# The last stage of an encoder block in program order, with operands made two steps ahead

## The chip, the cores and the metric

The kernel runs on one core of a Trainium2 chip. The metric is the device time of one execution in microseconds, the median of several. Besides, one execution is recorded by the profiler; its "span" runs from the first to the last instruction of the program. The engines are PE (TensorE, matmuls), DVE (VectorE), ACT (ScalarE), POOL (GpSimd) and SP (SyncE, which here only issues DMAs). Each engine works through its own instructions in the order that it was given, and waits at the first one that isn't ready.

## The reference, cut to what matters

One layer of an encoder: input norm, dilated attention and a recurrent branch, a merge, a norm, then SwiGLU and a last norm. The change lies in the very last product and that norm:

```python
D_MODEL = 1024; SEQ = 1024; D_FF = 2816        # all float32
def layer_norm(x, g, b):
    mu = mean(x); xc = x - mu
    return xc * rsqrt(mean(xc * xc) + 1e-5) * g + b
...
    h = layer_norm(alpha * h + merged @ w_o, ln1_g, ln1_b)
    gate, up = split(h @ w_ffn_in, 2)
    h = layer_norm(alpha * h + (silu(gate) * up) @ w_ffn_out, ln2_g, ln2_b)
```

In the last line a 1024 x 2816 matrix is multiplied by a 2816 x 1024 one.

## The kernel before, in words

**Precision.** A float32 operand is split into two float32r parts, hi and lo, with hi + lo the operand (`split`, L204 the cast, L208 the subtraction). A product of two split operands is three matmuls (`mm3`, L229 to L231): hi·hi, hi·lo, lo·hi. By default the cast is ACT's and the subtraction POOL's; for some tiles (`eng_lo="dve"`) it is DVE's.

**The last stage** (`ffn_out`) multiplies the activations g (rows by D_FF) with `w_ffn_out` in Strassen-Winograd form: each matrix is cut into 2 x 2 quarters, and seven products of sums of quarters replace eight. `OUT_ORDER` is the order of the first six, (1, 2, 6, 5, 7, 3); product 4 comes last in a loop of its own. The inner dimension of a quarter, 1408, is cut into NJ = 11 pieces of 128. A *step* is one product and one piece j: 12 matmuls (four row tiles t of 128 rows, three matmuls each) into four PSUM banks, X (`pj`) for products 1, 6, 7, 4 and Z (`sd`) for 2, 5, 3. There are 66 steps. The products accumulate on each other in the banks as the Winograd form asks: 6 on 1, 7 on 6, 4 on 7, 3 on 5.

**Operands of a step.** The activations of products 1, 2 and 6 (a11, a12, s2) lie in DRAM whole: one DMA (`graw`, three buffers under the tag `wsum`) and a split into `ghi`, `glo` (three buffers), cast on ACT, subtraction on DVE. Those of 5, 7 and 3 (s1, s3, s4) lie there split: two DMAs straight into `ghi` and `glo`. The weights come in four quarters b11, b12, b21, b22, 11 tiles of 128 x 512 (256 KB) each, and stay in SBUF. `right` makes a product's weight operand with DVE sums in place: nothing for products 1 and 2, b12−b11 and b22−b11 for 6, b21+b11 for 5 (kept for later; the operand is b11), b22−b12 for 7, b21−b22 for 3. `split` then makes `w_hi`, `w_lo` (four buffers) on ACT and POOL. During product 3 product 4's weights are split as well (`t4hi`, `t4lo`). Product 4's activations a22 come as two transfers of 704 KB per row tile (`a22h`, `a22l`), in two buffers each.

**Loads.** `at(step, ...)` hangs each bulk load on a step: weight tiles, the eight residual row tiles (`rows`, Y), the two vectors of the norm (`vector`), the first two pairs of a22 (`last_acts`). They are issued by SP, kept in program order by `queued`.

**Rows.** When a product's banks are complete, `add` adds them to the residual rows in Y, one addition per step or all at once. `finish(t)` normalises a row tile: statistics of both halves (DVE, `stats`), the power −1/2 (POOL), scale and shift (ACT, `normalise`), the multiplication by g2 (POOL, L1592), the addition of b2 (DVE, L1593) and the output DMA (L1594). Tile 7 does the last parts by halves on DVE (L1584, L1587).

**Order.** Outside what `queued` fixes, a scheduler orders each engine's instructions when the program is built: it goes by program order as priority and by its own estimate of when an instruction is ready. `add` runs in a block that raises its priority (`evac_ahead`).

**The last loop** (product 4), over t = 0 to 3: for t of 2 and 3 the a22 pair is loaded at the head of the turn; then 33 matmuls into X[t], the addition, and `finish` of three tiles in turns 0 and 1, of one in turns 2 and 3.

`out_begin`, called from the stage before, loads the first four weight tiles and three activations and splits step 0's operands.

Of the kernel before, what the change touches and what calls it, by code (L numbers as in the profile page):

```python
# [81 lines left out]
class Block:  # L82
# [1397 lines left out]
    OUT_ROWS = {1: ((0, 0),), 2: ((0, 0),), 6: ((0, 1),), 5: ((1, 1),), 7: ((1, 1),), 3: ((0, 1),)}  # L1480

    def queued(self, o, i):

        return self.tc.keep_in_program_order(self.nc.sync.dma_start(o, i))
# [4 lines left out]
    def out_block(self, t, n, j):  # L1489
        k, c = int(n[1]) - 1, int(n[2]) - 1  # L1490
        self.queued(t, self.wfo[128 * (j + NJ * k):128 * (j + NJ * k + 1), HALF * c:HALF * (c + 1)])
        return t

    def out_raw(self, p, j):
        r = self.ws.tile([128, HALF], F32, name="graw", tag="wsum", bufs=3)
        self.queued(r, self.gd[self.OUT_G[p]][j][0])
        return r

    def out_begin(self):
# [11 lines left out]
        self.begun = {(1, 0): (g, w)}  # L1511
        self.raws = {(1, j): self.out_raw(1, j) for j in (1, 2)}

    def ffn_out(self):


        nc = self.nc
        with ExitStack() as es:
            wb = es.enter_context(self.pool("fow"))
            rp = es.enter_context(self.pool("for", "right"))  # L1520
            W, Y, gains = self.W, {}, []
            halves = [slice(HALF * h, HALF * (h + 1)) for h in range(2)]

# [3 lines left out]
            def rows(t):  # L1527
                Y[t] = y = rp.tile([128, D], F32, name="y2", tag=f"y2{t}", bufs=1)
                self.queued(y, self.ahs_d[t])

            def vector(i):
                v = self.ln["2"][i]
                gains.append(rp.tile([128, D], F32, name=f"gb{i}"))
                self.queued(gains[i], bass.AP(tensor=v.tensor, offset=v.offset, ap=[[0, 128], [1, D]]))

            def acts(p, j):
                d = self.gd[self.OUT_G[p]][j]
                z = [rp.tile([128, HALF], F32R, name=f"g{n}", tag=f"g{n}", bufs=3) for n in ("hi", "lo")]
                if len(d) == 1:
                    self.split(*z, self.raws.pop((p, j), None) or self.out_raw(p, j), eng_lo="dve")  # L1540
                else:
                    for t, s in zip(z, d):
                        self.queued(t.bitcast(F32), s)
                return z

            a22 = []

            def last_acts(t, i):
                if i == 0:
                    a22.append([rp.tile([128, NJ, 128], F32R, name=f"a22{z}", tag=f"a22{z}", bufs=2) for z in "hl"])  # L1550
                self.queued(a22[t][i].bitcast(F32), self.gd["a22"][i][:, :, 128 * t:128 * (t + 1)])

            def right(p, j):
                b11, b12, b21, b22 = (W.get((n, j)) for n in ("b11", "b12", "b21", "b22"))
                if p == 1:
                    return b11
                if p == 2:
                    return b21
                if p == 6:
                    t2 = self.ws.tile([128, HALF], F32, name="wt2", tag="wkeep", bufs=3)  # L1560
                    nc.vector.tensor_sub(b11, b12, b11)
                    nc.vector.tensor_sub(t2, b22, b11)
                    return t2
                if p == 5:
                    nc.vector.tensor_add(b21, b21, b11)
                    return b11
                if p == 7:
                    nc.vector.tensor_sub(b12, b22, b12)
                    return b12
                nc.vector.tensor_sub(b21, b21, b22)  # L1570
                return b22

            def add(t, h, ps):
                with self.tc.high_priority(offset=self.evac_ahead):
                    nc.vector.tensor_add(Y[t][:, halves[h]], Y[t][:, halves[h]], ps)

            def finish(t):
                y, (g2, b2) = Y[t], gains
                mv = self.stats(rp, y, "2")
                if t == 7:  # L1580
                    for n in range(2):
                        for s in halves:
                            if n == 0:
                                nc.vector.scalar_tensor_tensor(y[:, s], y[:, s], mv[:, 0:1], g2[:, s],  # L1584
                                                               op0=OP.subtract, op1=OP.mult)
                            else:
                                nc.vector.scalar_tensor_tensor(y[:, s], y[:, s], mv[:, 2:3], b2[:, s],  # L1587
                                                               op0=OP.mult, op1=OP.add)
                                nc.sync.dma_start(self.out[128 * t:128 * (t + 1), s], y[:, s])
                else:  # L1590
                    self.normalise(rp, y, y, mv)
                    nc.gpsimd.tensor_mul(y, y, g2)  # L1592
                    nc.vector.tensor_add(y, y, b2)  # L1593
                    nc.sync.dma_start(self.out[128 * t:128 * (t + 1), :], y)  # L1594
# [22 lines left out]
            late, adds, step = {}, [], 0  # L1617
            for p in self.OUT_ORDER:
# [75 lines left out]
```

## Time and profile before

| | |
|---|---|
| timed runs | median 2212.6 us, 2210.78 to 2212.82 (3 runs) |
| profiled execution | 2210.36 us |
| its span | 2208.6 us |
| PE busy | 2048.6 us, 93% |
| DVE, ACT, POOL busy | 1380.7, 919.4, 1234.5 us |
| mean granted clock of PE | 0.97 |

The profile lists instructions by line of the kernel, engine and tile, with start times in us from the span's start. "Idle before, releaser" is the time that the engine had waited and what ended that wait. `pj` and `sd` are PSUM banks; `Wb` a weight tile, `w_raw` one of the first four; `wt` the sum b22−b11. SPq is SP's queue of DMA issues. Matmul durations overlap: the pace is read from the distances of starts.

### The profile page before, as it was taken

Reading aid. Unit: us, or ns where it says so; the run is one execution under the profiler, and the core shown is the slowest. Engines: PE = TensorE matmul, PEld = TensorE weight load, DVE = VectorE, ACT = ScalarE, POOL = GpSimd, SP = SyncE. Lnnn points to the kernel's source line nnn. Section 1 sums busy time; section 2 is a strip of 40 time slices with the busy share of each in tenths; the row PEclk is TensorE's granted clock in tenths of the full one; section 3 lists DMA queues with packets and bytes.
Section 4 is the critical chain, followed back from the end, with each engine's and each line's share of the span. In section 5 each row is a group of like instructions: output and inputs, shape, how many; then the busy total and the mean of one; then the engine's idle time right before and its main releaser. Section 6 shows DMA issues by size and latency. Waiting matters only on the chain.

```text
span 2208.6 us, 31268 instructions
## 1 busy us (share of the span) xinstructions
PE 2048.6 (93%) x10941; PEld 1685.4 (76%) x10941; DVE 1380.7 (63%) x2165; ACT 919.4 (42%) x1870; POOL 1234.5 (56%) x960
## 2 busy tenths in 40 slices
PE   4799999999999999999999999998999999988973
PEld 3678887878878888778887788786888888777862
DVE  7657645885378846776456323368688887767242
ACT  6534454433554445444553321344444344343220
POOL 3565653666446654556546653535677777555450
PEclk9899999999999999999999999999999999999996
DMA  5333442434333452435427562345344444484743
GB/s 204 103 121 106 155 137 93 137 127 154 118 109 129 131 162 92 136 116 161 133 82 270 191 210 82 125 133 181 124 154 163 146 164 151 156 288 137 244 150 96
DMA packets 296447, 324.20 MB, mean 147 GB/s; under 512 B 15905, under 2 KB 212834, under 8 KB 296290
## 3 DMA queue, kind: packets, MB, share of 16 engines
q1 hardware_dynamic: 288832, 296.81, 41.8%
q10 hardware_dynamic: 7458, 25.40, 3.0%
q8 instruction: 86, 1.41, 0.3%
q14 instruction: 71, 0.58, 0.1%
HBM read 211.78 MB, written 110.36 MB: 146 GB/s over the span
## 4 chain that ended last, share of the span: by engine, by line
PE 56%; DVE 8%; DMA 4%; issue 4%; POOL 4%; ACT 2%; SPq 0%; DVEq 0%; POOLq 0%; ACTq 0%
PE pj L229 12%; PE pj L231 12%; PE pj L230 12%; PE sd L231 5%; PE sd L229 5%; PE sd L230 5%; POOL w_lo L208 2%; PE sd L1023 1%; ACT p L801 1%; DMA a22l<-ga22l 1%; DVE p L823 1%; DVE y L1593 1%; DVE hR L984 1%; DMA wa<-in_w_in_dram 1%; DVE qd L938 1%
## 5 line engine op out<-in xcount | busy, mean ns | idle before, releaser
L208 POOL TENSOR_TENSOR w_lo<-wa,w_hi 128x512 fp32r<-128x512 f32 x276 | 387.2, 1411 | 278.9 <-ACT w_hi L204 271.3
L204 ACT CAST w_hi<-wa 128x512 fp32r<-128x512 f32 x276 | 170.1, 618 | 235.5 <-PE pj L230 169.4
L208 POOL TENSOR_TENSOR w_lo<-wsum,w_hi 128x512 fp32r<-128x512 f32 x88 | 135.6, 1551 | 78.0 <-ACT w_hi L204 41.2
L208 POOL TENSOR_TENSOR w_lo<-f_raw,w_hi 128x512 fp32r<-128x512 f32 x66 | 110.4, 1686 | 66.0 <-ACT w_hi L204 64.2
L229 PE MATMUL pj<-xt1hi,w_hi 128*128 128x512 f32 x268 | 108.9, 407 | 23.6 <-ACT xt1hi L204 16.7
L208 POOL TENSOR_TENSOR w_lo<-Wb,w_hi 128x512 fp32r<-128x512 f32 x47 | 72.5, 1545 | 73.5 <-ACT w_hi L204 71.9
L230 PE MATMUL pj<-xt1lo,w_hi 128*128 128x512 f32 x268 | 107.8, 402 | 4.5 <-DVE xt1lo L208 4.5
L231 PE MATMUL pj<-xt1hi,w_lo 128*128 128x512 f32 x268 | 107.1, 400 | 0.0
L231 PE MATMUL pj<-xb22hi,w_lo 128*128 128x512 f32 x268 | 105.0, 392 | 2.2 <-POOL w_lo L208 2.2
L229 PE MATMUL pj<-xb22hi,w_hi 128*128 128x512 f32 x268 | 105.9, 395 | 0.1
L463 POOL TENSOR_TENSOR wa<-wa,wa 128x512 f32<-128x512 f32 x46 | 64.5, 1403 | 72.3 <-DVE ws L462 59.8
L230 PE MATMUL pj<-xb22lo,w_hi 128*128 128x512 f32 x268 | 104.9, 391 | 0.0
L208 POOL TENSOR_TENSOR w_lo<-ws,w_hi 128x512 fp32r<-128x512 f32 x46 | 67.4, 1468 | 63.7 <-ACT w_hi L204 57.3
L485 ACT COPY wkeep<-pj 128x512 f32<-128x512 f32 x138 | 80.4, 583 | 11.4 <-DVE evh L377 5.9
L229 PE MATMUL pj<-xb11hi,w_hi 128*128 128x512 f32 x188 | 77.9, 416 | 5.1 <-DVE wkeep L402 3.6
L204 ACT CAST w_hi<-wsum 128x512 fp32r<-128x512 f32 x88 | 54.6, 620 | 63.9 <-PE sd L230 61.3
L388 DVE TENSOR_TENSOR evh<-wkeep,pj 128x512 f32<-128x512 f32 x48 | 32.6, 679 | 76.5 <-PE pj L231 56.4
L1393 ACT ACTIVATE fth<-fc 128x512 f32<-128x512 f32 x44 | 27.8, 633 | 125.9 <-DVE fc L1392 125.9
L229 PEld LDWEIGHTS pj<-xt1hi,w_hi 128*128 128x128 f32 x268 | 51.8, 194 | 37.1 <-ACT xt1hi L204 17.4
L231 PE MATMUL pj<-xt2hi,w_lo 128*128 128x512 f32 x188 | 74.7, 397 | 3.8 <-POOL w_lo L208 3.8
L229 PE MATMUL pj<-xt4hi,w_hi 128*128 128x512 f32 x188 | 75.9, 404 | 2.3 <-DVE evh L377 2.3
L975 ACT ACTIVATE hS<-hR,dec 128x128 f32<-128x128 f32 x112 | 44.5, 402 | 78.8 <-DVE hR L984 56.8
(416 smaller groups left out, 6717.2 us busy)
## 6 DMA issues: line engine op xcount, KB each, us to landing
wa<-in_w_in_dram SPq DMA_DIRECT2D x184, 256.0 KB, 3.0
f_raw<-in_w_ffn_in_dram SPq DMA_DIRECT2D x44, 512.0 KB, 4.3
Wb<-in_w_ffn_out_dram SPq DMA_DIRECT2D x40, 256.0 KB, 4.1
tg<-evh SPq DMA_DIRECT2D x32, 256.0 KB, 3.1
tg<-tg SPq DMA_DIRECT2D x16, 512.0 KB, 3.6
y<-ahs SPq DMA_DIRECT2D x16, 512.0 KB, 4.9
ah<-xt ACTq DMA_DIRECT2D x8, 512.0 KB, 6.6
rec<-hg ACTq DMA_DIRECT2D x8, 512.0 KB, 3.7
```

Of the source, the lines that this page charges most:

```text
L204: nc.scalar.copy(hi, src)
L208: e.tensor_sub(lo, src, hi.bitcast(F32))
L229: nc.tensor.matmul(ps, whi, xhi, start=first, stop=False, **kw)
L230: nc.tensor.matmul(ps, whi, xlo, start=False, stop=False, **kw)
L231: nc.tensor.matmul(ps, wlo, xhi, start=False, stop=last, **kw)
L388: nc.vector.tensor_add(t, add, ps)
L463: nc.gpsimd.tensor_sub(a["a21"], a["a11"], a["a21"])
L485: nc.scalar.copy(t, ps)
L801: nc.scalar.activation(z, z, AF.Exp, bias=N0[p, hd, tt:tt + 1], scale=QSCALE, accum_out=L0[p, hd, tt:tt + 1])
L823: nc.vector.tensor_scalar(z, z, W0[p, hd, tt:tt + 1], None, op0=OP.mult)
L975: nc.scalar.activation(S[:, c, :], E, AF.Copy, scale=dec[:, 1, c:c + 1])
L1393: nc.scalar.activation(th[:, s], c[:, s], AF.Tanh, scale=0.5)
```

## The change

Only the last stage is changed. What it computes, the number of instructions of each kind and their operands stay.

1. A context `in_order` chains all instructions traced inside it to the one before on the same engine, so that each engine follows program order through the whole stage; it takes the place of `queued` and of the raised priority of `add`.
2. A step's operands are made two steps ahead: in step s stand `sums(s + 2)` (its weight sum) and `prep(s + 2)` (its splits), then the bulk loads of step s, then the matmuls of step s, then one addition or statistics from the list `todo`, then the activation DMAs (`acts`) of step s + 4 where they come whole, of s + 3 where they come split.
3. The sum b12−b11 is made with product 2 in place of product 6.
4. Loads are hung on other steps: b21 at 4 + j (was 7 + j), b12 at 6 + j (16 + j), rows 0 to 3 from 15 (11), rows 4 to 7 from 32 (33), the first a22 pairs from 52 (55).
5. Statistics are taken per half: `stat(t, h)`. One half of each tile is taken between steps, after products 2 and 7; `moments` does the rest.
6. In the last loop the a22 pairs for t = 2 and 3 are issued right behind the matmuls of t = 0 and 1, ahead of those turns' outputs. `finish` returns the last addition and the output DMA as a function, which is called after the next tile's `finish`. The order of tiles is 0, 1, 4, 2, 3, 5, 6, 7.

```diff
+    @contextmanager
+    def in_order(self):
+        traced = self.nc.cur_bb.bb.instructions
+        n = len(traced)
+        yield
+        for i in traced[n:]:
+            before = self.lasts.get(i.engine)
+            if before is not None:
+                self.tc.add_manual_dep(i, before, mybir.DependencyInfo(mybir.DependencyClass.NoSync,
+                                                                       mybir.DependencyReason.DATA), reason="in_order")
+            self.lasts[i.engine] = i.name
...
+            def sums(s):
+                if not 0 <= s < len(steps):
+                    return
+                p, j = steps[s]
                 b11, b12, b21, b22 = (W.get((n, j)) for n in ("b11", "b12", "b21", "b22"))
-                if p == 1:
-                    return b11
                 if p == 2:
-                    return b21
-                if p == 6:
-                    t2 = self.ws.tile([128, HALF], F32, name="wt2", tag="wkeep", bufs=3)
                     nc.vector.tensor_sub(b11, b12, b11)
+                elif p == 6:
+                    W["t2", j] = t2 = self.ws.tile([128, HALF], F32, name="wt2", tag="wkeep", bufs=3)
                     nc.vector.tensor_sub(t2, b22, b11)
...
+            RIGHT = {1: "b11", 2: "b21", 6: "t2", 5: "b11", 7: "b12", 3: "b22"}
+
+            def prep(s):
+                if s >= len(steps) or s in ready:
+                    return
+                p, j = steps[s]
+                w = self.flat()
+                raw = self.raws.pop((p, j), None)
+                if raw is not None:
+                    g = pair()
+                    nc.scalar.copy(g[0], raw)
+                    nc.vector.tensor_sub(g[1], raw, g[0].bitcast(F32))
+                else:
+                    g = G.pop(s)
+                self.split(*w, W[RIGHT[p], j])
+                ready[s] = g, w
 
             def add(t, h, ps):
-                with self.tc.high_priority(offset=self.evac_ahead):
-                    nc.vector.tensor_add(Y[t][:, halves[h]], Y[t][:, halves[h]], ps)
+                nc.vector.tensor_add(Y[t][:, halves[h]], Y[t][:, halves[h]], ps)
+
+            def stat(t, h):
+                if t not in S:
+                    S[t] = rp.tile([128, 2, 6], F32, name="bns", tag=f"bns{t}", bufs=1)
+                nc.vector.bn_stats(S[t][:, h, :], Y[t][:, halves[h]])
...
+                self.normalise(rp, y, y, mv)
+                nc.gpsimd.tensor_mul(y, y, g2)
+                return lambda: (nc.vector.tensor_add(y, y, b2),
+                                nc.sync.dma_start(self.out[128 * t:128 * (t + 1), :], y))
...
             for j in range(NJ):
-                at(7 + j, load, "b21", j)
-                at(16 + j, load, "b12", j)
+                at(4 + j, load, "b21", j)
+                at(6 + j, load, "b12", j)
                 at(17 + j, load, "b22", j)
             for t in range(4):
-                at(11 + t, rows, t)
-                at(33 + 2 * t, rows, 4 + t)
+                at(15 + t, rows, t)
+                at(32 + 2 * t, rows, 4 + t)
             for i in range(2):
                 at(46 + 2 * i, vector, i)
                 for t in range(2):
-                    at(55 + 4 * t + 2 * i, last_acts, t, i)
+                    at(52 + 4 * t + 2 * i, last_acts, t, i)
...
+            with self.in_order():
+                acts(3)
+                prep(1)
+            for s, (p, j) in enumerate(steps):
                 bank = X if p in (1, 6, 7) else Z
-                for j in range(NJ):
-                    if (p, j) in self.begun:
-                        g, w = self.begun[p, j]
-                    else:
-                        g, w = acts(p, j), self.flat()
-                        self.split(*w, right(p, j))
-                    for f, *a in bulk.pop(step, []):
+                with self.in_order():
+                    sums(s + 2)
+                    prep(s + 2)
+                    for f, *a in bulk.pop(s, []):
                         f(*a)
-                    if p == 3:
-                        late[j] = ...
+                    if p == 3 and j:
+                        later(j - 1)
+                    g, w = ready.pop(s)
                     for t in range(4):
                         c = slice(128 * t, 128 * (t + 1))
                         self.mm3(bank[t], g[0][:, c], g[1][:, c], *w, ...)
-                    if adds and (p != 2 or j > 4):
-                        add(*adds.pop(0))
+                    if todo and (p != 2 or j >= NJ - 4):
+                        f, *a = todo.pop(0)
+                        f(*a)
+                    acts(s + (4 if steps[min(s + 4, len(steps) - 1)][0] in (1, 2, 6) else 3))
+                if j == NJ - 1:
+                    i, h = self.OUT_ROWS[p]
+                    adds = [(add, 4 * i + t, h, bank[t]) for t in range(4)]
+                    todo += adds
+                    if p in (2, 7):
+                        todo += [(stat, 4 * i + t, h) for t in range(4)]
...
+            with self.in_order():
+                later(NJ - 1)
+                for f, *a in todo:
+                    f(*a)
+                for t in range(4):
+                    for j in range(NJ):
+                        self.mm3(X[t], A[t][0][:, j, :], A[t][1][:, j, :], *late[j], False, j == NJ - 1, ...)
+                    if t < 2:
+                        for i in range(2):
+                            last_acts(2 + t, i)
+
+                    def done(r):
+                        ends.append(finish(r))
+                        if len(ends) > 1:
+                            ends.pop(0)()
+
+                    if t == 0:
+                        for r in range(4):
+                            stat(r, 1)
+                        done(0)
+                        done(1)
+                    if t == 1:
+                        done(2)
+                        done(3)
+                    add(4 + t, 0, X[t])
+                    stat(4 + t, 0)
+                    if t < 3:
+                        done(4 + t)
+                    else:
+                        ends.pop(0)()
+                        finish(7)
```

More of the change, by code (lines that the diff above doesn't have):

```diff
@@ L1 @@
 import math
-from contextlib import ExitStack
+from contextlib import ExitStack, contextmanager
 import numpy as np
@@ L1520, in ffn_out @@
             rp = es.enter_context(self.pool("for", "right"))
-            W, Y, gains = self.W, {}, []
+            W, Y, S, V, G, A, ready = self.W, {}, {}, [], {}, [], self.ready
             halves = [slice(HALF * h, HALF * (h + 1)) for h in range(2)]
+            steps = [(p, j) for p in self.OUT_ORDER for j in range(NJ)]
             def load(n, j):
@@ L1536, in acts @@
[L1536 removed]
+                V.append(rp.tile([128, D], F32, name=f"gb{i}"))
+                nc.sync.dma_start(V[i], bass.AP(tensor=v.tensor, offset=v.offset, ap=[[0, 128], [1, D]]))
+            def acts(s):
+                if s >= len(steps):
+                    return
+                p, j = steps[s]
                 d = self.gd[self.OUT_G[p]][j]
[L1538 removed]
                 if len(d) == 1:
[L1540 to L1544 removed]
@@ L1546, in ffn_out, with pair @@
-            a22 = []
+                    if (p, j) not in self.raws:
+                        self.raws[p, j] = self.out_raw(p, j)
+                    return
+                G[s] = z = pair()
+                for t, v in zip(z, d):
+                    nc.sync.dma_start(t.bitcast(F32), v)
+            def pair():
+                return [rp.tile([128, HALF], F32R, name=f"g{n}", tag=f"g{n}", bufs=3) for n in ("hi", "lo")]
             def last_acts(t, i):
                 if i == 0:
-                    a22.append([rp.tile([128, NJ, 128], F32R, name=f"a22{z}", tag=f"a22{z}", bufs=2) for z in "hl"])
-                self.queued(a22[t][i].bitcast(F32), self.gd["a22"][i][:, :, 128 * t:128 * (t + 1)])
@@ L1553, in right @@
-            def right(p, j):
+                    A.append([rp.tile([128, NJ, 128], F32R, name=f"a22{z}", tag=f"a22{z}", bufs=2) for z in "hl"])
+                nc.sync.dma_start(A[t][i].bitcast(F32), self.gd["a22"][i][:, :, 128 * t:128 * (t + 1)])
+            def sums(s):
+                if not 0 <= s < len(steps):
+                    return
+                p, j = steps[s]
                 b11, b12, b21, b22 = (W.get((n, j)) for n in ("b11", "b12", "b21", "b22"))
-                if p == 1:
-                    return b11
@@ new lines, in add, with moments @@
+            def add(t, h, ps):
+                nc.vector.tensor_add(Y[t][:, halves[h]], Y[t][:, halves[h]], ps)
[3 more added lines that the diff above has]
+                nc.vector.bn_stats(S[t][:, h, :], Y[t][:, halves[h]])
+            def moments(t):
+                mv = self.tiny.tile([128, 4], F32, name="mv2", tag="bnmv", bufs=3)
+                nc.vector.bn_aggr(mv[:, 0:2], S[t])
+                nc.vector.tensor_scalar(mv[:, 2:3], mv[:, 1:2], LN_EPS, None, op0=OP.add)
+                nc.gpsimd.tensor_tensor(mv[:, 2:3], mv[:, 2:3], self.mhalf[:, 0:1], OP.pow)
+                return mv
@@ L1577, in finish @@
             def finish(t):
-                y, (g2, b2) = Y[t], gains
-                mv = self.stats(rp, y, "2")
+                y, (g2, b2) = Y[t], V
+                mv = moments(t)
                 if t == 7:
[L1581 to L1594, printed above, removed]
+                    for s in halves:
+                        nc.vector.scalar_tensor_tensor(y[:, s], y[:, s], mv[:, 0:1], g2[:, s], op0=OP.subtract,
+                                                       op1=OP.mult)
+                    for s in halves:
+                        nc.vector.scalar_tensor_tensor(y[:, s], y[:, s], mv[:, 2:3], b2[:, s], op0=OP.mult, op1=OP.add)
+                        nc.sync.dma_start(self.out[128 * t:128 * (t + 1), s], y[:, s])
+                    return
```

62 lines of the change are left out of this document (21 added, 41 removed).

## The prediction

> **What bounds the kernel now.** I read the page first, then PE's busy time by stretch, then PE's waits in the last stage, then the timelines of PE, DVE, ACT, POOL and SP there. The profiled execution took 2210.36 us, its span 2208.6 us (1.8 us around it); the three timed runs have a median of 2212.6. Of change and no change this measurement can tell 0.2% apart, about 4.4 us. The last stage runs from about 1928 to the end.
>
> ```profile
> span 2208.6 us, 31268 instructions
> ...
> 1928.60:1980.00 51.40, 51.36 (x217) 41.65 (x217) 28.99 (x41) 21.77 (x39) 24.20 (x16) 0.97 0.83 283
> 1980.00:2030.00 50.00, 36.54 (x144) 28.65 (x144) 46.95 (x58) 15.48 (x27) 33.17 (x14) 0.90 0.41 131
> 2030.00:2125.50 95.50, 95.50 (x423) 79.09 (x422) 16.05 (x25) 24.32 (x40) 43.07 (x33) 1.00 0.75 245
> 2125.50:2208.60 83.10, 36.09 (x132) 27.56 (x130) 34.61 (x55) 8.36 (x7) 23.56 (x15) 0.71 0.27 85
> ```
>
> The columns are length, busy time of PE, weight loads, DVE, ACT and POOL, clock, DMA share and GB/s. The reader sees two holes in PE: 13.5 us idle in the second stretch, where DVE is busy 46.95 of 50 us, and 47 us in the last, where the clock also falls to 0.71. The third stretch is full: nothing but fewer matmuls could shorten it. Who ended the waits:
>
> ```profile
> PE pj L229 <- DMA a22h<-ga22h: 37.0, 2, 22.4
> PE sd L230 <- POOL w_lo L208: 6.9, 1, 6.9
> PE pj L231 <- DVE glo L208: 6.5, 3, 3.8
> PE pj L229 <- ACT ghi L204: 3.3, 1, 3.3
> ```
> ```profile
> 1928.64 0.67 PE L229 MATMUL pj<-w_hi,ghi 128*128 128x512 f32 x1 [3.31 <-ACT ghi L204]
> ...
> 1933.09 0.39 PE L229 MATMUL pj<-w_hi,ghi 128*128 128x512 f32 x1
> ...
> 1987.00 0.79 PE L230 MATMUL sd<-w_lo,ghi 128*128 128x512 f32 x1 [6.92 <-POOL w_lo L208]
> ...
> 2030.02 0.39 PE L229 MATMUL pj<-w_hi,ghi 128*128 128x512 f32 x1
> ...
> 2139.95 0.39 PE L231 MATMUL pj<-t4hi,a22l 128*128 128x512 f32 x1
> 2162.73 0.77 PE L229 MATMUL pj<-t4hi,a22h 128*128 128x512 f32 x1 [22.39 <-DMA a22h<-ga22h]
> ...
> 2200.44 0.39 PE L231 MATMUL pj<-t4hi,a22l 128*128 128x512 f32 x1
> ```
>
> Between 2030.02 and 2139.95 lie 485 steady matmuls: 109.93 / 485 = 0.2267 us each, so a step of 12 takes 2.72 us and a block of 33 (product 4, one row tile) 7.5 us. Between 1933.09 and 2030.02 the timeline has 348 matmul starts, worth 78.9 us at that pace; 96.9 passed. **Lost in the middle: 18.0 us**, the waits on `w_lo` and `glo` and the half clock behind them. Let E be the time at which the sixth product has issued: 66 matmuls of product 4 come before 2140.18, so E = 2140.2 − 15.0 = 2125.2. **From E to the end: 83.4 us**, for only 132 matmuls (29.9 us).
>
> **The change, part by part.** *The middle.* DVE, POOL and ACT now take their work step by step. The instruction count is the same (five weight sums, one split and 12 matmuls a step), so the question is whether a step's operands, made two steps ahead, are ready. One step's chain in before:
>
> ```profile
> 1946.79 0.62 ACT L204 CAST ghi<-graw 128x512 fp32r<-128x512 f32 x1 [1.20 <-PE pj L230]
> 1947.32 0.61 ACT L204 CAST w_hi<-Wb 128x512 fp32r<-128x512 f32 x1
> ...
> 1947.45 0.69 DVE L208 TENSOR_TENSOR glo<-graw,ghi 128x512 fp32r<-128x512 f32 x1 [1.66 <-ACT ghi L204]
> ...
> 1948.01 1.29 POOL L208 TENSOR_TENSOR w_lo<-Wb,w_hi 128x512 fp32r<-128x512 f32 x1 [1.06 <-ACT w_hi L204]
> ```
>
> From 1946.79 to 1949.30 is 2.5 us. In the new order the chain of step s+2 starts when step s−1 frees its buffers (three for `ghi`, `glo`) and must end two steps, 5.44 us, later: 2.9 us spare. DVE has per step at most a sum, a split and an addition or statistics (3 × 0.6 = 1.8 us), POOL 1.29, ACT two casts of 0.52, all below 2.72. The sum b12−b11, moved from the third product to the second, is what keeps it at one sum a step. I take the whole 18.0 us as gone; if the cover fails, all or part stays. What was wrong before:
>
> ```profile
> L208 POOL TENSOR_TENSOR w_lo<-Wb,w_hi x47: 1284/1294/10182, 1933.4 to 2117.5; 128x512 fp32r<-128x512 f32 x47
> ```
> ```profile
> 1977.32 0.68 DVE L1561 TENSOR_TENSOR w_raw<-Wb,w_raw 128x512 f32<-128x512 f32 x1
> ...
> 1985.15 0.68 DVE L1570 TENSOR_TENSOR Wb<-Wb,Wb 128x512 f32<-128x512 f32 x1
> ```
>
> Fourteen DVE instructions followed each other every 0.60 us, sums for products far ahead among them, and one `w_lo` took 10.18 us instead of 1.29. The page "SBUF — State Buffer" of the Trainium skill (section "Who interferes with whom") says that a two-input DVE instruction and a GpSimd one exclude each other, and that the loser waits until the first has finished. By that rule one `w_lo` would wait for one instruction, 0.68 us, and the lockout below could not come back at all; the trace shows a wait through fourteen, so I keep that rival.
>
> *The loads.* b21 comes 3 steps earlier, b12 ten earlier, rows 0–3 four later, rows 4–7 one earlier, the first two a22 pairs three earlier; all go through SP in program order, where the next activations wait for a buffer and hold up what is behind. The first stretch moved 283 GB/s at a share of 0.83: 341 at full share. Steps 4–18 ask for 50 pieces of 0.262 MB in 40.8 us, 321 GB/s; steps 15–18 alone for 386. They fall behind by (386 − 341) × 10.9 / 341 = 1.4 us. An activation is issued some 1.5 us into the step three before its split, 6.7 us ahead, and
>
> ```profile
> Wb<-in_w_ffn_out_dram SPq DMA_DIRECT2D x40, 256.0 KB, 4.1
> ...
> a22l<-ga22l SPq DMA_DIRECT2D x4, 704.0 KB, 7.6
> ```
>
> a piece of that size lands in 4.1: 2.6 us spare against 1.4. Cost nothing; without cover 1.4 us, at worst a few such. The additions of product 1 (steps 18–21) read the banks that product 6 writes from step 22; late rows would stop PE there. From product 5 on operands come already split, three buffers as before, and the full third stretch says that this suffices; costed at nothing, behind the same depth.
>
> *The beginning.* In before the casts of w_hi for steps 1–3 ran by 1923.8, ahead of the first `ghi`; in program order `ghi` comes first.
>
> ```profile
> 1923.15 0.62 ACT L204 CAST w_hi<-w_raw 128x512 fp32r<-128x512 f32 x1 [0.60 <-issue]
> 1927.45 0.62 ACT L204 CAST gh<-s 128x512 fp32r<-128x512 f32 x1 [3.68 <-DVE s L1430]
> 1927.97 1.13 ACT L204 CAST ghi<-graw 128x512 fp32r<-128x512 f32 x2
> ```
>
> If `ghi` cannot come before 1927.97 (it stands behind the last cast of the stage before), w_lo of step 1 ends 2.5 us later, at 1930.5, instead of PE starting at 1928.64: +1.8 us. The bounds are −3.3 (PE's whole wait goes) and +3; I take +1.8, since the releaser of 1927.45 belongs to the stage before and doesn't change.
>
> *The end.* Before, SP had the last two a22 pairs behind the output rows:
>
> ```profile
> 2148.71 7.77 DVE y L1593 x3
> ...
> 2156.92 0.53 SPq L1484
> 2157.55 7.45 DMA a22l<-ga22l
> ```
>
> so they went out at 2156.92, 16.7 us after the matmuls had stopped. Now the pair for t=2 stands ahead of the outputs and goes when t=0 has left its buffer, E+7.8; 8.1 us later (2156.92 to 2165.04, the end of that transfer) it is there, E+15.9, against PE ready at E+15.0. The same again for t=3: PE ends at E+30.9 and loses 1 us instead of 37. With the last addition's 0.4 us and
>
> ```profile
> 2200.87 0.69 DVE L1575 TENSOR_TENSOR y<-y,pj 128x512 f32<-128x512 f32 x1 [17.44 <-PE pj L231]
> ...
> 2202.70 1.40 DVE L1584 SCALAR_TENSOR_TENSOR y<-y,mv,gb 128x512 f32<-128x512 f32 x2
> ```
>
> the 7.7 us from there to the span's end, PE alone would end the kernel at E+39.0. **What is late next** is the row normalisation. POOL in program order does pow(0), multiply(0), pow(1), multiply(1)…, and tile k+1's ACT step needs pow(k+1): tiles run one behind the other. One tile's turn, from tile 6 of before, which ran alone:
>
> ```profile
> 2176.01 1.29 DVE L194 BATCH_NORM_STATS2 bn<-y 128x6 f32<-128x512 f32 x2
> 2177.22 0.19 DVE L196 BATCH_NORM_AGGREGATE mv<-bn 128x2 f32<-128x12 f32 x1
> ...
> 2177.74 0.55 POOL L198 TENSOR_TENSOR mv<-mv,mhalf 128x1 f32<-128x1 f32 x1 [23.48 <-DVE mv L197]
> ...
> 2178.52 1.24 ACT L252 ACTIVATE y<-y,mv 128x1024 f32<-128x1024 f32 x1 [28.55 <-DVE mv L251]
> ...
> 2179.83 2.34 POOL L1592 TENSOR_TENSOR y<-y,gb 128x1024 f32<-128x1024 f32 x1 [1.54 <-ACT y L252]
> ...
> 2182.21 1.23 DVE L1593 TENSOR_TENSOR y<-y,gb 128x1024 f32<-128x1024 f32 x1 [3.72 <-POOL y L1592]
> ```
>
> From pow at 2177.74 to 2182.21: 4.47 us. The first pow: last addition at E+0.2, then four statistics at 0.6 us, aggregate, 0.5 us: E+3.85. Seven tiles: E+35.1. Behind DVE's wait for each pow stand the addition of the tile before and product 4's next addition; only output transfers wait for those, until the last tile. Then tile 6's addition 1.23, tile 7's aggregate and scalar step 0.3 and from 2202.70 to 2208.6 another 5.9: **E+42.6**, 3.6 us behind PE's own end. The half of the statistics made early (16 × 0.6 us, half of them) is what lets the chain begin at E+3.85.
>
> *Costed at nothing:* the dropped priority of the additions (each has its own step, 0.6 us on a DVE below 2.0 of 2.72); the last t4 split (ACT, DVE ahead of the last additions, made while step 65 multiplies; uncovered 1.3 us).
>
> **Sum against the profiled execution:** 2208.6 + 1.8 − 18.0 − (83.4 − 42.6) = 2151.6 span, plus 1.8: **2153 us**.
>
> **Rivals.** *Lockout again* (the middle keeps its stall). In steps 20–30 POOL's 1.29 and DVE's two two-input instructions (1.2) fill 2.5 of 2.72 us. For it: the 10.18 row. Against it: split and cast wait on PE's progress every step, so DVE cannot run ahead. Half to all of the 18 us stays: 2162 to 2171.
> *Loads late at the end.* SP's pair for t=3 stands behind output row 1, ready at E+14.9; its buffer frees at E+15.3. Were the chain of rows later by 10 us, PE's end would follow it, 2157 to 2163.
> *Better.* The beginning's wait vanishes, or pows slip so that tiles overlap, 2.4 us each by POOL: PE's E+39.0 decides: 2145 to 2149.
> *Slower, one mechanism.* Program order makes POOL's w_lo the pace: it decides from a mean of 2.72 us. The three of 1976.77 took 13.56, 4.52 each; at that pace 65 steps cost 65 × 1.8 = 117 us, 2270; at 3.6 us a step the gain is just eaten. Against it: the third stretch, where 33 POOL instructions took 43.07 us, 1.3 each.
> ```profile
> 1976.77 13.56 POOL L208 TENSOR_TENSOR w_lo<-Wb,w_hi 128x512 fp32r<-128x512 f32 x3 [3.53 <-ACT w_hi L204]
> ```
> *No effect:* the order written is the one already run: 2212. Against it: sums far ahead of their step at 1977.
>
> **Numbers.** Forecast 0.64 (own range 2147 to 2160), lockout 0.17, late loads 0.07, better 0.07, slower 0.03, no effect 0.02. The range 2144 to 2171 holds all but the last two and parts of the rivals. Faster 0.95, same 0.02, slower 0.03.
>
> **What would show it.** Right: no DVE run of sums ahead of its step; w_lo at 1.3 to 2.0 us; PE full from 1934 to E near 2109; a22 pairs issued as t=0 and t=1 end, PE's waits on them about 1 us each; POOL's multiplies 4.5 us apart in the tail, and the end set by the chain of rows, not PE. Wrong: PE gaps between 1934 and E on `w_lo` or on activations, or pows 2.4 us apart.

## The result, and the profile after

The changed kernel took 2150.8 us (median of 4 runs, 2146.2 to 2156.3) against 2212.0 for the kernel before in the same set: a ratio of 0.9725, 95% interval 0.970 to 0.975. The profiled execution took 2148.89 us, its span 2147.1. The forecast was 2153 (2144 to 2171): right in the whole, with one term of the sum wrong.

The page's first line and PE's busy time in stretches of the last stage (columns as before: length, busy time of PE, weight loads, DVE, ACT and POOL, clock, DMA share, GB/s):

```profile
span 2147.1 us, 31283 instructions
...
1928.60:1980.00 51.40, 51.40 (x227) 42.49 (x227) 34.02 (x34) 21.70 (x38) 23.74 (x19) 0.99 0.89 300
1980.00:2030.00 50.00, 50.00 (x222) 41.42 (x221) 42.20 (x48) 16.93 (x29) 27.43 (x20) 1.00 0.57 189
2030.00:2106.00 76.00, 75.66 (x330) 61.03 (x330) 40.50 (x47) 20.65 (x35) 33.88 (x24) 1.00 0.74 232
2106.00:2147.10 41.10, 29.35 (x129) 23.64 (x127) 21.66 (x46) 8.72 (x7) 21.23 (x15) 0.92 0.53 173
```

The second stretch is full now: 50.00 of 50 us, 222 matmuls where before had 144. What is idle lies in the last 41 us. All that PE still waited for from 1900 on (engine and line, what it waited for, us in total, times, longest):

```profile
PE pj L229 <- ACT w_hi L204: 3.2, 1, 3.2
PE pj L230 <- POOL w_lo L208: 0.9, 1, 0.9
PE pj L231 <- DMA a22l<-ga22l: 0.9, 1, 0.9
PE sd L229 <- DMA ghi<-gs4h: 0.3, 1, 0.3
```

The 37.0 us on `a22h` and the 6.9 and 6.5 on `w_lo` and `glo` are gone. To lay runs beside each other I cut each trace at four points of PE's timeline, by counting matmuls: 25 ahead of the first that reads `ghi` ("cut"; behind it come the end of the stage before and most of step 0, whose operands bear the names `w_hi` and `w_lo`); that first one, with which step 1 begins; the first of step 2, 12 matmuls later; and E, where 780 have issued from step 1 on, as many as steps 1 to 65 have. "Middle" is from step 2 to E; 768 matmuls at 0.2267 us would be 174.1. "Tail" is from E to the span's end. There is one profiled execution of each kernel.

| kernel | cut at | to first ghi | to step 2 | middle | tail | PE's last from E | span |
|---|---|---|---|---|---|---|---|
| before | 1915.6 | 13.1 | 17.5 | 192.1 | 83.3 | 75.2 | 2208.6 |
| after | 1914.7 | 9.1 | 14.7 | 175.6 | 42.1 | 30.9 | 2147.1 |
| e1_queue_kept | 1912.8 | 11.1 | 17.2 | 175.2 | 42.1 | 31.3 | 2147.3 |
| e3_loads_back | 1909.0 | 9.1 | 14.6 | 175.6 | 76.3 | 67.3 | 2175.5 |
| e5_sum_back | 1912.7 | 9.1 | 14.6 | 180.3 | 42.1 | 31.0 | 2149.7 |
| e6_no_chain | 1915.6 | 15.6 | 20.9 | 207.1 | 42.3 | 30.4 | 2185.8 |
| e7_no_ahead | 1911.2 | 9.1 | 15.3 | 177.8 | 42.1 | 30.9 | 2146.5 |
| e8_sp_chain_only | 1912.9 | 14.8 | 20.1 | 191.1 | 47.6 | 38.5 | 2171.7 |
| e9_stats_late | 1914.5 | 9.1 | 15.0 | 175.2 | 45.9 | 36.3 | 2150.8 |
| e4_pow_ahead | 1928.1 | 9.2 | 15.2 | 176.2 | 41.1 | 32.5 | 2160.5 |
| e10_rows_ahead | 1910.2 | 9.1 | 14.7 | 175.4 | 47.6 | 39.6 | 2147.9 |
| e11_small_pad | 1925.4 | 9.2 | 15.5 | 175.7 | 42.1 | 31.8 | 2158.7 |
| e12_pairs_first | 1912.9 | 9.1 | 14.7 | 175.4 | 45.0 | 30.9 | 2147.9 |
| e13_seven_first | 1909.1 | 9.1 | 14.7 | 175.6 | 42.2 | 31.0 | 2141.6 |

The 61.5 us of span split, but for rounding, into 0.8 ahead of the cut, 2.8 at the beginning (17.5 to 14.7), 16.6 in the middle and 41.2 in the tail. The first column has to be read before any span: apart from e4 and e11 these kernels have the same instructions up to that point but for the place of a few loads and casts, and still reach it anywhere from 1909.0 to 1915.6. A span that differs by less than some 7 us says nothing of the last stage; its segments do.

What the middle's operands look like now, the groups of `w_lo` and of two of the five weight sums (engine, operation, count: shortest, median and longest ns, first and last start):

```profile
L208 POOL TENSOR_TENSOR w_lo<-Wb,w_hi x47: 1289/1294/1836, 1930.6 to 2095.0; 128x512 fp32r<-128x512 f32 x47
...
L1574 DVE TENSOR_TENSOR Wb<-Wb,Wb x7: 1202/1795/1796, 1957.8 to 1974.8; 128x512 f32<-128x512 f32 x7
L1577 DVE TENSOR_TENSOR wt<-Wb,Wb x7: 1190/1193/1197, 1988.4 to 2004.7; 128x512 f32<-128x512 f32 x7
```

Before, POOL's longest `w_lo` was 10.18 us; now it is 1.84, and DVE pays most of it instead, 1.19 or 1.79 us for a sum of 0.68. The sums of a product run from its beginning to its end, one a step, none in a burst.

And the tail, the end of the chain that ended last, in order of time (start, us, what):

```profile
2130.89 0.56 POOL mv L1614
2131.45 0.02 issue
2131.47 0.17 DVE mv L251
2131.64 0.02 issue
2131.66 1.25 ACT y L252
2132.92 0.07 issue
2132.99 1.66 POOL y L1629
2134.64 0.69 issue
2135.34 0.56 POOL mv L1614
```

pow, scale, ACT, multiplication, next pow: one tile's turn is 4.45 us, and no PE is in it. SP's queue ahead of it:

```profile
2112.42 0.52 SPq L1566 DMA_DIRECT2D a22h<-ga22h  x1
2113.00 0.69 SPq L1566 DMA_DIRECT2D a22l<-ga22l  x1
2114.98 4.80 SPq L1631 DMA_DIRECT2D out_dram<-y  x2
2119.90 0.52 SPq L1566 DMA_DIRECT2D a22h<-ga22h  x1
```

Both pairs go out where t=0 and t=1 end (E+7.5 and E+14.9), the second right behind two output rows.

### The profile page after: what moved, and what is told of

Its sections match the earlier page's. It is cut to its first block, busy times and chain, and to the rows that moved or that the text cites. A ratio compares the mean times of both kernels' runs of the same rounds, so it can differ in the third digit from the quotient of the medians.

```text
span 2147.1 us, 31283 instructions
## 1 busy us (share of the span) xinstructions
PE 2032.1 (95%) x10941; PEld 1675.5 (78%) x10941; DVE 1394.1 (65%) x2165; ACT 918.8 (43%) x1870; POOL 1214.0 (57%) x960
## 3 DMA queue, kind: packets, MB, share of 16 engines
q8 instruction: 86, 1.41, 0.3%
## 4 chain that ended last, share of the span: by engine, by line
PE 59%; DVE 5%; issue 4%; DMA 4%; POOL 3%; ACT 2%; SPq 0%; DVEq 0%; ACTq 0%; POOLq 0%
PE pj L229 12%; PE pj L230 12%; PE pj L231 12%; PE sd L231 5%; PE sd L229 5%; PE sd L230 5%; POOL w_lo L208 2%; PE sd L1023 1%; ACT p L801 1%; DVE p L823 1%; DMA wa<-in_w_in_dram 1%; POOL y L1629 1%; DVE hR L984 0%; DMA binb<-in_ln_in_b_dram 0%; PE sd L628 0%
## 5 line engine op out<-in xcount | busy, mean ns | idle before, releaser
L208 POOL TENSOR_TENSOR w_lo<-ws,w_hi 128x512 fp32r<-128x512 f32 x46 | 67.3, 1468 | 63.6 <-ACT w_hi L204 63.2
L208 POOL TENSOR_TENSOR w_lo<-Wb,w_hi 128x512 fp32r<-128x512 f32 x47 | 64.7, 1376 | 65.5 <-ACT w_hi L204 64.3
L462 DVE TENSOR_TENSOR ws<-wa,wa 128x512 f32<-128x512 f32 x46 | 39.3, 856 | 60.6 <-DMA wa<-in_w_in_dram 42.3
```

Source lines behind the costliest of these rows:

```text
L208: e.tensor_sub(lo, src, hi.bitcast(F32))
L462: nc.vector.tensor_add(a["s1"], a["a21"], a["a22"])
```

## The experiments

Each is an edit of the changed kernel, unless it says otherwise. They ran in four sets, each with its own runs of the kernel before (medians 2210.1, 2211.2, 2208.7 and 2207.9).

**The order: e6_no_chain.** In the last stage no engine is held to program order.

```diff
-            before = self.lasts.get(i.engine)
+            before = None
```

> The changed kernel without the chain: in_order adds no dependence, so the scheduler may order all engines by its own estimate; the text of the program is the same. Theory 'chain': DVE makes sums ahead of their step again, splits come late or POOL is locked out, and 9 to 18 us of the middle's loss return: span 2156 to 2166. Rival 'listing': the scheduler takes program order as its priority, so the new listing alone gives nearly the same order: 2146 to 2150.

Measured: 2185.4 us (2182.8 to 2187.6), ratio 0.9888 (0.9873 to 0.9904), longer than either forecast. Its first stretch, PE's longest wait, and the weight loads, first of e6, then of the changed kernel:

```profile
1928.60:1980.00 51.40, 29.81 (x108) 23.26 (x108) 33.00 (x40) 13.13 (x22) 14.22 (x10) 0.77 1.04 373
```
```profile
PE pj L229 <- ACT ghi L1595: 36.9, 4, 21.3
```
```profile
L1500 SPq DMA_DIRECT2D Wb<-in_w_ffn_out_dram x40: 327/332/1148, 1925.7 to 1963.8; - x40
```
```profile
L1500 SPq DMA_DIRECT2D Wb<-in_w_ffn_out_dram x40: 328/430/1387, 1920.3 to 1993.7; - x40
```

Forty weight loads leave SP in 38 us instead of 73. They move at 373 GB/s with a DMA share of 1.04, and the activations come behind them: PE stands 36.9 us for `ghi`. The middle is 207.1, worse than before the change. So in this code the chain on SP is what paces the loads (e8, which has it alone, has a middle of 191.1). The tail keeps its gain (42.3) without the chain.

**e8_sp_chain_only.** Program order on SP alone.

```diff
+            if i.engine != mybir.EngineType.SP:
+                continue
```

> The changed kernel with the chain on SP's DMAs alone; DVE, ACT, POOL and PE are left to the scheduler. Without any chain the middle (step 2 to E) took 207 us instead of 175.6, with all weight loads issued by 1964 and activations waiting behind them. Theory 'SP alone': the order of the loads is all that counts, the middle is 176 to 179 us and the span 2147 to 2151. Rival 'DVE too': the scheduler puts sums ahead of their step as in before, and part of the 16.6 us lost there returns: middle 183 to 195 us, span 2155 to 2167.

Measured: 2173.3 us (2171.9 to 2175.2), ratio 0.9836 (0.9817 to 0.9855). Its second stretch and PE's waits:

```profile
1980.00:2030.00 50.00, 40.35 (x158) 31.79 (x159) 49.43 (x63) 17.76 (x31) 21.14 (x14) 0.93 0.44 142
```
```profile
PE pj L229 <- ACT ghi L1597: 9.0, 1, 9.0
PE pj L231 <- DVE glo L1598: 6.0, 3, 4.2
PE sd L231 <- DVE glo L1598: 4.9, 4, 2.3
```

DVE is busy 49.43 of 50 us: sums for products 7 and 3 run from 1982 on, 67 us and more ahead of their steps, and `glo` waits. The middle, 191.1, is that of the kernel before (192.1). So the order on the engines other than SP is what ends the stall; that DVE's is the one that counts is read from these rows, not tried by itself. That order also matters at both ends: without it step 2 comes 5.4 us later from the cut (20.1 against 14.7), and the tail is 5.5 us longer (47.6).

**e7_no_ahead.** The order kept, but sums and operands are listed in their own step instead of two steps ahead.

```diff
-                    sums(s + 2)
-                    prep(s + 2)
+                    sums(s)
+                    prep(s)
```

> The changed kernel with sums and splits listed in their own step instead of two steps ahead (program order kept on every engine; activation loads as in the changed kernel). Theory 'buffers': ACT and POOL have the same order either way and run ahead as far as their buffers let them; only DVE's additions now stand ahead of the next two steps' splits, which costs about 1 us at the few boundaries between products: span 2148 to 2153. Rival 'two steps': the listing two steps ahead is what covers the 2.5 us chain; without it a step's operands come some 1 us late in many of the 66 steps: 2175 or more.

Measured: 2148.4 us (2146.0 to 2152.3), ratio 0.9723 (0.9705 to 0.9742). The middle is 177.8, 2.3 us above the changed kernel's; most of it is one gap in the last step of product 6 (`w_hi` 1.0 and `w_lo` 0.85 near 2010). Being listed ahead hardly matters. That each engine runs ahead as far as its buffers allow, wherever the lines stand, is the theory that fits; the waits show no more than that.

**e5_sum_back.** b12−b11 goes back from product 2 to product 6, beside b22−b11.

> The changed kernel with b12-b11 made again with product 6: none in product 2's steps, two sums in each of product 6's. In the changed kernel DVE idles 0.32 us in each of these 2.72 us steps, and its sums take 1.2 us beside POOL. Theory 'room': another 0.6 to 1.2 us per step doesn't fit; DVE's step becomes 3.0 to 3.6 us for 11 steps, 3 to 10 us less the 2.9 us of lead: middle 0 to 7 us longer, most likely 3, span 2147 to 2154. Rival 'covered': the sums have no wait on PE, run in DVE's gaps and the lead covers the rest: middle 175 to 176 us as before.

Measured: 2150.9 us (2149.3 to 2155.2), ratio 0.9737 (0.9719 to 0.9756), by time not to be told from the changed kernel. The middle is 180.3 against 175.6, 4.8 us more, and the waits say where:

```profile
PE pj L230 <- POOL w_lo L208: 3.2, 7, 0.9
```

One of the seven is step 1's 0.9, which the changed kernel has too. The other six are the last steps of product 6: with two sums a step beside POOL's `w_lo` they come 3.35 us apart or more, instead of 2.72. The moved sum is worth 4.8 us, shown by the segments alone.

**The end: e3_loads_back.** The a22 pairs for t=2 and t=3 are issued ahead of their own matmuls, behind the outputs, as before.

```diff
+                    if t >= 2:
+                        for i in range(2):
+                            last_acts(t, i)
...
-                    if t < 2:
-                        for i in range(2):
-                            last_acts(2 + t, i)
```

> The changed kernel, but the a22 pairs for turns 2 and 3 stand again at the head of their turns, behind the outputs of the turns before. Theory: SP holds them behind the outputs, whose rows come 4.45 us apart: the pair for turn 2 goes out at E+28, PE idles some 21 us; that for turn 3 waits for tile 5's output, near E+49, PE idles again some 10 us; with half clock after each idle time the end moves from E+42 to about E+75, the span from 2147 to about 2180. Rival: the turn's place doesn't matter, since the buffer frees at the same time anyway and SP runs ahead: 2147 to 2150.

Measured: 2180.7 us (2177.3 to 2182.6), ratio 0.9866 (0.985 to 0.9881). Tail 76.3, PE's last matmul at E+67.3:

```profile
PE pj L229 <- DMA a22h<-ga22h: 28.6, 2, 18.5
...
PE pj L231 <- DMA a22l<-ga22l: 2.3, 2, 1.2
```

So, with the new order of rows, 34.2 of the tail's 41.2 us come from where four loads stand on SP.

**e9_stats_late** (timed once). The 16 early row statistics go back behind the last additions.

> The changed kernel with all statistics in the last loop: for tiles 0 to 3 both halves (eight of 0.6 us instead of four) ahead of the first aggregate, for tiles 4 to 7 both halves behind the addition. If the chain of rows sets the end, the first pow starts 2.4 us later and the tail grows from 42.1 to 44.5 us, and tile 7's second half adds 0.6 us only if it is not hidden by the wait for tile 6. If PE sets the end, the tail grows by 0.6 us alone.

Measured: 2152.5 us, tail 45.9: 3.8 us more instead of the 2.4 expected. The first pow and SP's pair for t=3:

```profile
2110.84 0.55 POOL L1614 TENSOR_TENSOR mv<-mv,mhalf 128x1 f32<-128x1 f32 x1 [14.65 <-DVE mv L1613]
```
```profile
2117.20 4.82 SPq L1631 DMA_DIRECT2D out_dram<-y  x2
2122.11 0.52 SPq L1566 DMA_DIRECT2D a22h<-ga22h  x1
```
```profile
PE pj L231 <- DMA a22l<-ga22l: 3.1, 1, 3.1
```

pow comes at E+6.0 instead of E+3.7, the 2.4 us expected. But output row 1 is then later too, the pair for t=3 goes out behind it at E+17.3 instead of E+14.9, and PE, now last, adds the rest. This is the rival "loads late at the end": a small delay of the rows sets it off.

**The beginning: e1_queue_kept.** The loads of the stage's beginning are held in SP's program order again.

```diff
+        if self.beginning:
+            self.tc.keep_in_program_order(i)
```

> The changed kernel, but the seven loads of out_begin (four weight tiles, three activations) are again kept in SP's program order, as before the change. The two profiles differ at the start of the last stage: step 2 starts at 1929.4 instead of 1933.1. Theory 'loads': this comes from the loads, which without their queue went out early (weights at 1396 instead of 1912); then step 0 waits for them again, step 2 starts near 1933 to 1935, and the span is 2151 to 2153. Rival 'collision': in before POOL made three w_lo at 1920 while DVE made the last sums of the stage before (1.7 us each instead of 0.7), and program order puts these w_lo behind the first ghi; then the late loads disappear in PE's idle time of 3.2 us at 1920 and the span changes by less than 1 us (2147 to 2148).

Measured: 2152.8 us (2149.1 to 2155.2), ratio 0.974 (0.9724 to 0.9755); the span is that of the changed kernel to 0.2 us. Read by that alone, the loads would be worth nothing. But e1 came to the cut 1.9 us earlier and reached step 2 after 17.2 us instead of 14.7: 2.5 us lost, nearly all that the beginning had gained. The loads, of before, of the changed kernel, and a wait that e1 has and the changed kernel has not:

```profile
L1484 SPq DMA_DIRECT2D w_raw<-in_w_ffn_out_dram x4: 430/431/439, 1912.0 to 1913.9; - x4
```
```profile
L1500 SPq DMA_DIRECT2D w_raw<-in_w_ffn_out_dram x4: 328/384/427, 1395.8 to 1398.8; - x4
```
```profile
1914.83 0.50 PE L229 MATMUL pj<-w_hi 128*128 128x512 f32 x1 [1.68 <-ACT w_hi L204]
```

**Versions beyond the change.** As the tail is one tile after another, I tried to overlap tiles.

*e4_pow_ahead* makes the four pows ahead of the four multiplications, in small tiles of their own.

> The changed kernel with another order in the last loop: the aggregates and pows of tiles 0 to 3 come before their multiplications on POOL, and the last additions of rows stand where their multiplication has ended; nothing else. Theory 'chain of rows': the changed kernel ends 42.1 us after E because POOL does pow and multiplication of one tile after the other, 4.45 us a tile, while PE has ended at E+30.9. With pows ahead the multiplications follow each other every 2.4 us and PE decides the end: last matmul at E+31, then 7.7 to 8.2 us, so a tail of 39 us, 3 us less; span near 2144. Rival 'multiplications or outputs': the tail is set by the seven multiplications with the last additions and outputs as such, and stays at 42 us.

Measured: 2160.5 us (2159.4 to 2162.3), ratio 0.9779 (0.9763 to 0.9794). Slower, but not in the tail (41.1). It came to the cut at 1928.1, 13 us late, with no instruction changed up to there. And in the tail the overlap is paid for:

```profile
2127.67 9.06 POOL L1624 TENSOR_TENSOR y<-y,gb 128x1024 f32<-128x1024 f32 x3
```
```profile
2129.07 9.87 DVE L1627 TENSOR_TENSOR y<-y,gb 128x1024 f32<-128x1024 f32 x4
```

These rows merge instructions that met with some that ran alone. One by one, the two multiplications that ran beside additions took 3.4 us instead of 2.4, and the three additions beside them 2.1 to 3.4 instead of 1.22.

*e11_small_pad* asks where the 13 us come from: the changed kernel with its instructions in the same order, and only the tile for mean and variance under a tag of its own with six buffers, 96 bytes more a partition.

> The changed kernel, every instruction the same and in the same order, but the moments of the last stage lie under a tag of their own: 96 bytes more in the pool of small tiles, which shifts what is allocated behind it. Theory 'addresses': the matmuls of the stage before the last come every 0.2333 us instead of 0.2267 as in the first try of pows ahead, some 13 us in all, span near 2160. Rival 'run': that try was slow for another reason (its chip, its order), and this kernel runs like the changed one, 2147 to 2151.

Measured: 2161.0 us (2159.6 to 2162.9), ratio 0.9784 (0.9765 to 0.9804): most of e4's loss, from 96 bytes. 200 us of the stage before, in the changed kernel and in e11:

```profile
1700.00:1900.00 200.00, 199.93 (x877) 163.86 (x876) 167.03 (x152) 83.13 (x148) 145.16 (x90) 1.00 0.46 152
```
```profile
1700.00:1900.00 200.00, 200.00 (x859) 161.12 (x858) 167.53 (x149) 81.07 (x143) 138.83 (x88) 1.00 0.46 154
```

Same instructions, on PE in the same order from the kernel's first to its last, full clock, PE never idle, and 859 matmuls instead of 877: they follow each other every 0.2333 us instead of 0.2267. All matmuls of that stretch are slowed alike, whatever tile they read. The slow pace holds, in e4 as in e11, from about 1263 us to the last stage, and neither ahead of that nor behind. It isn't the chip: e10 ran on the same one as e11 and has 877.

*e10_rows_ahead* is e4 with mean and variance kept in the tile of the statistics, and with two or three multiplications in a row between the pows.

> The changed kernel with the last loop ordered so that a row tile's moments and scaling come as early as their data: moments of tiles 0 to 3 first, those of 4, 5 and 6 right behind their addition and ahead of the multiplications that remain. The moments lie in the statistics' own tile of the last stage, so that no tile of an earlier stage moves (in the first try of pows ahead the small tiles took 96 bytes more, and the matmuls of the stage before came every 0.2333 us instead of 0.2267). Theory 'chain of rows': PE decides the end, tail 39 to 40 us instead of 42.1, span 2 to 3 us shorter at the same start of the stage. Rival 'port': DVE's additions of b2 and POOL's multiplications slow each other (2.47 and 2.85 us instead of 1.2 and 2.4 where they met in the first try), and the tail stays at 41 to 42 us.

Measured: 2151.4 us (2149.6 to 2157.0), ratio 0.9744 (0.9723 to 0.9764). The cut is reached at 1910.2: the shift is gone. But the tail is 47.6, which neither theory had. SP, and PE's wait:

```profile
2117.23 3.68 SPq L1630 DMA_DIRECT2D out_dram<-y  x2
2121.00 0.52 SPq L1566 DMA_DIRECT2D a22h<-ga22h  x1
```
```profile
PE pj L229 <- DMA a22h<-ga22h: 4.4, 1, 4.4
```

*e12_pairs_first* is e10 with both pairs ahead of all outputs on SP.

> e10_rows_ahead with one thing moved: on SP both remaining a22 pairs (t=2 and t=3) now stand ahead of all output rows; rows 0 and 1 leave behind them. Counted from E, the end of the sixth product. Theory 'output row 1 on SP' (e10's lateness came from the pair for t=3 queued behind output row 1): the pair goes out as soon as t=1 has left its buffer, about E+15.3, PE loses 1 us instead of 4.4 + the half clock behind it, PE's last matmul comes at about E+30.5 instead of E+39.6. The kernel's end then follows DVE's order: tile 6's b2 addition (E+37.5 in e10) stands ahead of tile 7's last addition, and 7.7 us from there make a tail of about 45 (47.6 in e10, 42.1 in after). Rival 'DVE and POOL alone' (the pair was late only because everything on DVE was late, and PE follows DVE): PE's last matmul stays near E+39, tail 47 to 48. In both cases no faster than the changed kernel by more than drift.

Measured: 2151.1 us (2149.7 to 2153.8), ratio 0.9742 (0.9716 to 0.9769). PE's last matmul moves from E+39.6 to E+30.9, the tail from 47.6 to 45.0, as the theory "output row 1 on SP" had it. The other 2.9 us above the changed kernel's lie, by its rows, in DVE's order, where tile 7's last addition stands behind tile 6's; that was not tried by itself.

*e13_seven_first* is the changed kernel with tile 7's first scalar step ahead of tile 6's last addition.

```diff
-                        ends.pop(0)()
-                        finish(7)
+                        finish(7, ends.pop(0))
```

> The changed kernel with one edit at the very end: tile 7's mean, variance and first scalar step (two instructions) stand ahead of tile 6's b2 addition on DVE, so that they run while POOL still multiplies tile 6; pow of tile 7 stands behind that multiplication in both. Theory 'the chain of rows sets the end': behind tile 6's multiplication come now its addition (1.23) and tile 7's second scalar step (1.41) instead of addition, aggregate 0.3, first step 1.41 and second step 1.41: 1.5 to 1.7 us off the tail, 42.1 to about 40.5. Rival 'the two engines exclude each other': the two scalar steps beside POOL's multiplication cost the one or the other what they save, tail 41.5 to 42.5. In time 0.07% or nothing, under the run-to-run drift, so that it is read from the tail.

Measured: 2145.2 us (2143.5 to 2146.2), ratio 0.9711 (0.9689 to 0.9732). The lowest median, but it came to the cut at 1909.1; its tail is 42.2, the changed kernel's. DVE's end there:

```profile
2133.42 2.02 DVE L1622 SCALAR_TENSOR_TENSOR y<-y,mv,gb 128x512 f32<-128x512 f32 x2
2135.36 1.21 DVE L1631 TENSOR_TENSOR y<-y,gb 128x1024 f32<-128x1024 f32 x1
2136.50 1.40 DVE L1626 SCALAR_TENSOR_TENSOR y<-y,mv,gb 128x512 f32<-128x512 f32 x2
```

Beside POOL's multiplication the two scalar steps take 2.02 us instead of 1.41, and tile 6's addition starts at E+35.9 instead of E+34.8. The last step comes 0.6 us earlier (E+37.1 against E+37.6), and the end not at all, since three output transfers now leave within 1.3 us instead of 2.9 and the last one ends 0.6 us later after its issue (3.7 against 3.1 us). No version tried is shown to beat the changed kernel.

## Why the prediction was right, and where it was not

**The tail** (predicted 42.6, measured 42.1). Every step held: pairs out as t=0 and t=1 end, PE's last matmul at E+30.9 (E+30.9 predicted) with 0.9 us lost, first pow at E+3.7 (E+3.85), 4.45 us a tile (4.47). That the chain of rows sets the end and not PE is shown by e12, where PE ends at the same E+30.9 and the tail is 2.9 us longer; e3 shows how close PE comes behind: there PE ends 36 us later and the tail is 34 longer. PE alone would have given E+39.0, so the two are 3 us apart: e9 and e10 each tipped it.

**The middle** (18.0 us predicted to go, 16.6 went). Right in mechanism: e8 has DVE's sums ahead of their step and the old middle. The term was 1.4 us too large; 1.5 us remain above full pace, in gaps of 0.5 us and less. The cover was thinner than predicted: DVE's step was put at 1.8 of 2.72 us, and in product 6 DVE, its sums slowed beside POOL, idles only 0.32 us a step. So the sum moved off product 6, taken as a precondition, is one: 4.8 us without it.

**The beginning** (predicted +1.8 with bounds −3.3 and +3, measured −2.8): the step that failed. "If `ghi` cannot come before 1927.97": its releaser does belong to the stage before, but that one stands behind PE's last matmul there, and PE got to it sooner. PE, of before and then of the changed kernel:

```profile
1918.00 0.50 PE L229 MATMUL pj<-w_hi 128*128 128x512 f32 x1 [2.06 <-ACT w_hi L204]
...
1924.94 0.39 PE L231 MATMUL sd<-xt4hi,w_lo 128*128 128x512 f32 x1
```
```profile
1920.15 0.39 PE L231 MATMUL sd<-xt4hi,w_lo 128*128 128x512 f32 x1
1923.77 0.50 PE L229 MATMUL pj<-w_hi,ghi 128*128 128x512 f32 x1 [3.24 <-ACT w_hi L204]
```

From that last matmul to the first that reads `ghi` it is 3.7 us before and 3.6 now: PE's wait there, which the bound −3.3 would have removed, stays. The gain lies ahead of it, in the 24 matmuls behind the cut: 9.4 us before, 7.5 in e1, 5.4 in the changed kernel, which is full pace. Among them are step 0's. Before, they waited 2.06 us for a `w_hi` whose weight tile SP had loaded only at 1912, and from 1918.6 on the granted clock was 0.5 for 3.4 us. Holding the loads back again costs e1 2.0 of these 4.0 us. The other 1.9 are a somewhat shorter wait and full clock in e1's 24 matmuls; its clock is halved only later, from 1923.0 through step 1, and why then stays open. The prediction left out that dropping the queue frees four weight loads to go 500 us earlier.

Before, there was also a collision: POOL made three `w_lo` beside the last sums and splits of that stage on DVE. One of these sums, of before and of the changed kernel, and POOL before:

```profile
1919.31 1.65 DVE L1428 TENSOR_TENSOR s<-fc 128x512 f32<-128x512 f32 x1
```
```profile
1917.04 0.69 DVE L1428 TENSOR_TENSOR s<-fc 128x512 f32<-128x512 f32 x1
```
```profile
1920.38 5.12 POOL L208 TENSOR_TENSOR w_lo<-w_raw,w_hi 128x512 fp32r<-128x512 f32 x3
```

It cost little, as PE itself was late: `ghi`'s cast came 3.0 us behind that last matmul, against 2.4 in the changed kernel and in e1. With PE early it would have counted. In e8, which has the early loads but these `w_lo` first again, the cast that releases `ghi` (`gh`) comes 4.7 us behind that matmul instead of 1.9, and ACT then waits 2.9 us more at a `w_hi` for a later step whose tile is still on its way. So the early loads pay only together with the order on the other engines. The mechanism that the prediction did price is there: step 1 takes 5.63 us instead of 4.45 (6.12 in e1); its late `w_lo` is worth +1.2 of the +1.8.

**The rivals.** Lockout: not seen. By the page "SBUF — State Buffer" of the Trainium skill (section "Who interferes with whom") the second of the two to issue waits for the first to finish. The sums' 1.79 us, 0.68 and less than one `w_lo` of 1.29, agree with that; before's `w_lo` through fourteen DVE instructions does not, and the measurement decides there. Late loads: not in the changed kernel, but one small delay away (e9, e10). No effect and POOL's pace: excluded by the middle's 175.6.

In the total the errors partly cancelled: of the 4.5 us by which the span came out below the forecast's 2151.6, the beginning gave 4.6, the tail 0.4 and the part ahead of the cut 0.8, and the middle took 1.4.

## What to carry to other kernels

Look at what each in-order queue holds behind a waiting instruction: here 34 of 61 us were four loads behind output rows, and two later changes of the rows (e9, e10) met the same queue again. When an edit removes an ordering, list what else it frees, in the stage before too. And when early parts of a run drift by several us, compare segments that start with the same number of matmuls left, not times. A named instruction is not enough: the last matmul that reads `xt3hi` has two of step 0's matmuls ahead of it in the changed kernel, six in e6 and e8, and none before.

## What was not expected of the hardware

96 bytes more in one pool made all matmuls of the stage before come 0.2333 us apart instead of 0.2267 (859 against 877 in 200 us), at granted clock 1.00, about 11 us in all. That the cause is where tiles lie is the likeliest reading, but no run moves a tile by itself. The same page of the Trainium skill, in the same section, lists PE's ports as shared with no other engine; what slows PE here stays open.

Who loses when DVE and POOL meet is not fixed either: before, one POOL instruction waited through fourteen of DVE; with the engines in step both wait, DVE more often. From 1930 us to E in the changed kernel 44 of 118 two-input DVE instructions (128x512) took 1.2 to 1.8 us instead of 0.68, and 16 of 62 `w_lo` 1.4 to 1.8 instead of 1.29.
